# A hybrid encoder layer on one core: first transfers reordered, products of ones ahead of the data, rstd rows by way of DRAM, HGRN scores of two blocks issued together

## The chip, the cores and the metric

The kernel runs on one core of a Trainium2 chip. TensorE (PE) multiplies, VectorE (DVE), ScalarE (ACT) and GpSimd (POOL) do elementwise work, and SyncE (SP) issues the DMAs. The metric is the device time in microseconds of one execution; the median of the kernel before is 2376.36 us.

## The reference, cut to what matters

One layer is applied to two sequences, a prompt of 512 tokens and a sample of 1024. The model width is 1024, everything is float32.

```python
h = rms_norm(x, n_pre_mix)
proj = h @ w_in                       # width 6672
qkv_g, z_g, a_g, b_g, q_h, f_h, i_h, g_h, gate_raw = split(proj)
# branch A: bidirectional gated delta rule, 4 heads of 128, conv of 5 taps, chunks of 64
o_a = gated_delta(q, k, v, g[0], beta[0]) + flip(gated_delta(flipped ...))
y_a = (rms_norm(o_a) * silu(z_g)) @ w_br_gdn
# branch B: bidirectional HGRN2, 4 heads of 128
o_b = gla(qh, kh[0], ih, logf[0]) + flip(gla(flipped ...))
y_b = (rms_norm(o_b) * silu(g_h)) @ w_br_hg
merged = sigmoid(gates_0) * y_a + sigmoid(gates_1) * y_b
x = x + rms_norm(merged @ w_out, n_post_mix)
h2 = rms_norm(x, n_pre_ffn)
ff = (silu(h2 @ w_gate) * (h2 @ w_up)) @ w_down
return x + rms_norm(ff, n_post_ffn)
```

`gla` multiplies decayed queries and keys of one chunk into a triangular score matrix, applies it to the values, and carries a state from chunk to chunk.

## The kernel before, in words

**Tiles and stages.** The tokens form three blocks of 512: block 0 is the first sequence, blocks 1 and 2 are the second. Activations lie with features on the partitions, as eight 128x512 tiles per block (KD = 8). A product in full precision is made of three fp32r products of split operands: hi by hi, hi by lo, lo by hi. ACT rounds to the high part, DVE subtracts to get the low one (`split`). The mixer (projections, both branches, gates) takes about the first half of the span, then come the output projection and the feed-forward part, whose products use a seven-product Strassen scheme.

**An order written by a planner.** The program is first written as a tape. `Plan.run` interleaves five streams (prelude, GDN, HGRN, dense projections, output) by estimated times; a stream yields a time or a key and goes on when the plan has reached it. `Tape.schedule` (line 436) then simulates a list scheduler over the tape: each operation has a cost (line 289), an earliest time `o.rel` (0 at first, line 443) and a priority (its place on the tape), and each engine takes the ready operation of the best priority. It also assigns the buffers. `emit` (line 2599) writes the program in that order, and on the chip every engine runs its own list in order, with semaphores between engines.

**Units of small products.** `units` (line 416) binds products of the same small form into units that are emitted in one go. Line 423 lets an operation join the current unit only while the unit has newly opened at most two PSUM tiles (one, for full-size fp32 products). Lines 552 to 562 hold a unit of small products back by the number of instructions that PE was given in the last FETCH = 5000 ns: four for each fp32 product, two for others. With 64 products, a unit waits until the rest of the window holds at most 64.

**The start.** `layer` (line 766) loads the table of ACT (line 768) and makes the constants: `ones`, `ident`, masks; `vcol`, the 128x88 vector constants with all the gains, is loaded on SP (line 911). `prelude` (line 1155) then loads, for k = 0 to 7, the x tile and the w_ih tile (the HGRN value weights), each 256 KB, all on SP. With the entries of AHEAD (line 49) it also fetches 512 KB chunks of w_in early. `values(k)` (line 1180) converts x (scaled by the gain `g_mix`, a column of vcol) and w and multiplies them into four PSUM tiles, 12 products per k. After the first VSPLIT = 4 of them on the tape, `constants` and `ab_constants` follow (line 1193), small chains on DVE, ACT and POOL. The squares for the rms norm and their sums come next, at plan time TOKENS. Until rstd is known, projections use the unscaled x and are scaled when they are evicted; from plan time NORMED the x tiles are normalized one by one.

**rstd rows.** For blocks 1 and 2, `rstd_row` (line 1107) squares token rows, gets rstd as a column per 128 tokens, and spreads it to all partitions with four products ones x diag(y) on PE and a copy by ACT.

**HGRN.** `hg_stream` (line 1781) calls `hg_attn` (line 1793) for each head. For one block after the other it prepares four score operands per direction (`hg_pre`), multiplies the scores in 64 small products (16 of 32 rows by 64, 48 of 32 by 32, written to the PSUM tiles `pa` and `pb`), makes the state increments (`hg_post`) and selects the valid scores into SBUF. A small product is two instructions in the profile, so one block's burst has 128.

**Fillers.** `gates` (line 1731) and `dense_stream` (line 1743) give projections that can run at any time. HOLD (line 42) says how many gate chunks of a group go out early and how many wait for the inversion of the delta rule, MSTEP (line 43) at which of its steps that inversion counts as done.

Of the kernel before, what the change touches and what calls it, by code (L numbers as in the profile page):

```python
# [13 lines left out]
F32 = mybir.dt.float32  # L14
# [26 lines left out]
WBUFS = (2, 2, 2)  # L41
HOLD = ((2, 2, 1, 2), (2, 2, 2, 2))
MSTEP = (24, 28)
PAIR = False
# [3 lines left out]
NVEC = 88  # L48
AHEAD = {4: 512, 6: 1536, 7: 2064}
VSPLIT = 4  # L50
TRIG = 0
TOKENS, NORMED = 22.0, 30.0
QSQ = P * EPS ** 0.5
# [3 lines left out]
class Op:  # L57

    __slots__ = ("idx", "eng", "meth", "args", "kw", "occ", "dur", "tiles", "need", "succ", "rel", "prio", "form", "unit",
                 "asked", "port", "part")  # L60
# [103 lines left out]
class Tape:  # L164
# [29 lines left out]
    def __init__(self, nc):  # L194
        self.nc = nc
        self.fake = bacc.Bacc("TRN2", target_bir_lowering=False, num_devices=1)
        for n in self.ENGS:
            setattr(self, n, Tape.Eng(self, n))
        self.ops = []
        self.vts = {}  # L200
        self.pools = {}
        self.masks = {}
        self.cuts = {}
        self.count = 0
        self.part = (0, False)
        self.shift = 0

    def apart(self, pairs=False):
# [4 lines left out]
    @contextmanager  # L213
    def sooner(self, n):

        self.shift += n
        yield
        self.shift -= n

    def cut(self, name):  # L220
# [137 lines left out]
    def add(self, eng, meth, args, kw):  # L358
        o = Op()
        o.idx = len(self.ops)  # L360
        o.prio = o.idx - self.shift
        o.eng, o.meth, o.args, o.kw = eng, meth, args, kw
        o.form, o.unit, o.port, o.part = None, [o], 0, self.part
        out = args[0]
# [71 lines left out]
    def schedule(self):  # L436
# [4 lines left out]
        for o in ops:  # L441
            o.succ = []
            o.rel = 0.0
            o.asked = False
# [321 lines left out]
def layer(ctx, tc, x_p, x_s, w_out, n_post_mix, n_post_ffn, w_down, vec, xt_p, xt_s, w_in, w_br, w_gate, w_up,  # L766
# [52 lines left out]
    def dma(out, in_, eng=None):  # L819
        (eng or nc.sync).dma_start(out, in_)  # L820
        pl.dma(out, in_)
# [64 lines left out]
    def ctile(shape, name, dtype=F32):  # L886
        return const.tile(shape, dtype, name=name, tag=name)

    ident = ctile([P, P], "ident")
    nc.gpsimd.memset(ident, 0.0)  # L890
    nc.gpsimd.affine_select(ident, ident, [[-1, P]], ALU.not_equal, 1.0, base=0, channel_multiplier=1)
    ones = ctile([P, P], "ones")
    nc.vector.memset(ones, 1.0)
    ones_r = nc.tile(rpool, [P, P], F32R, "ones_r")
    eps_c = ctile([P, 1], "eps_c")
# [12 lines left out]
    for j in range(4):  # L908
        nc.gpsimd.memset(mbd[32 * j:32 * j + 32, 32 * j:32 * j + 32], 1.0)
    vcol = ctile([P, NVEC], "vcol")  # L910
    dma(vcol, vec)
    sgn, bwd, own, inc = [ctile([P, 1], n) for n in ("sgn", "bwd", "own", "inc_")]
# [194 lines left out]
    def rstd_row(blk_):  # L1107
# [13 lines left out]
        tt(y, y, u, ALU.mult)  # L1121
        pb = px()
        for t in range(4):
            dg = sblk("dg")
            ts(dg, ident, y[:, t:t + 1], ALU.mult)
            mm(t4(pb)[:, t, :], ones, dg)
        row = blk("row")
        copy(row, pb)
        rstd[blk_] = row
        yield 0  # L1130

    rstd = {}
    waiting = []

# [20 lines left out]
    def prelude(q):  # L1155
# [9 lines left out]
        if q.si == 0:  # L1165
            xt = []
            hi, lo = h_tiles()
            pv = [px() for t in range(4)]
            wr = []
            for k in range(KD):  # L1170
                xt.append(load(0, k))
                wr.append(blk("wv"))
                dma(wr[k], w_ih[k])
# [619 lines left out]
    def hg_attn(q, h):  # L1793
        out = q.hg[h]
        for b in range(q.nb):
            pa = px()
            pb = px()
            parts = [{}, {}]
            yield from par(*[hg_pre(h, out, b, d, parts[d]) for d in range(2)])
            pav, pbv = t4(pa), pb[:, 0:P].rearrange("p (t c) -> p t c", c=32)  # L1800
            halves = [slice(0, 64), slice(64, P)]
            yield pl.at(parts[0]["l64"], parts[1]["l64"], parts[0]["l32"], parts[1]["l32"])
            for t in range(4):
                for j in range(4):
                    d, sl = j // 2, slice(32 * j, 32 * j + 32)
                    dl = t4(parts[d]["l64"])
                    mm(pav[sl, t, halves[1 - d]], dl[:, t, sl], dl[:, t, halves[1 - d]])
            for d in range(2):
                e1, e2, l32 = [parts[d][n] for n in ("e1", "e2", "l32")]
                for t in range(4):  # L1810
                    for j in range(4):
                        sl = slice(32 * j, 32 * j + 32)
                        fs = slice(t * P + 32 * j, t * P + 32 * j + 32)
                        mm(pav[sl, t, sl] if d == 0 else pbv[sl, t, :], e2[:, fs], e1[:, fs])
                    for j in (0, 2):
                        ks, qs = [slice(32 * (j + z), 32 * (j + z) + 32) for z in (d, 1 - d)]
                        mm(pav[ks, t, qs], t4(l32)[:, t, ks], t4(l32)[:, t, qs])
# [4 lines left out]
            nc.vector.copy_predicated(av, m_all[:, None, :].to_broadcast([P, 4, P]), t4(pa))  # L1822
            pl.op("DVE", a_, [pa, a_])
            bd = sblk("bd").rearrange("p (t c) -> p t c", c=32)
            pset(bd, 0.0)
            nc.vector.copy_predicated(bd, m_b[:, None, :].to_broadcast([P, 4, 32]),
                                      pb[:, 0:P].rearrange("p (t c) -> p t c", c=32))
            pl.op("DVE", bd, [pb, bd])
            for j in range(4):
# [828 lines left out]
```

## Time and profile before

| what | us |
|---|---|
| median of 3 runs (2375.31 to 2376.83) | 2376.36 |
| the profiled execution | 2376.19 |
| its span, first to last instruction | 2374.5 |
| PE busy (14168 products) | 2359.3 |
| DVE busy | 1722.2 |
| ACT busy | 1244.3 |
| POOL busy | 753.7 |

The page gives busy times over the whole span. Products overlap on PE, and their ends are modelled, so the mean duration of a product is longer than the distance between two starts; how fast PE goes is read from counts in a window. Nearly all instructions have line 650, the planner's emit helper, so groups are told apart by their tiles: `bank` is PSUM, `ha` and `wa` hold split operands, `la`, `ba`, `sm`, `sa` are arenas of smaller tiles (`ones` lies in `sm`).

### The profile page before, as it was taken

Reading aid. Unit: us, or ns where it says so; the run is one execution under the profiler, and the core shown is the slowest. Engines: PE = TensorE matmul, PEld = TensorE weight load, DVE = VectorE, ACT = ScalarE, POOL = GpSimd, SP = SyncE. Lnnn points to the kernel's source line nnn. Section 1 sums busy time; section 2 is a strip of 40 time slices with the busy share of each in tenths; the row PEclk is TensorE's granted clock in tenths of the full one; section 3 lists DMA queues with packets and bytes.
Section 4 is the critical chain, followed back from the end, with each engine's and each line's share of the span. In section 5 each row is a group of like instructions: output and inputs, shape, how many; then the busy total and the mean of one; then the engine's idle time right before and its main releaser. Section 6 shows DMA issues by size and latency. Waiting matters only on the chain.

```text
span 2374.5 us, 37882 instructions
## 1 busy us (share of the span) xinstructions
PE 2359.3 (99%) x14168; PEld 1974.5 (83%) x14168; DVE 1722.2 (73%) x2826; ACT 1244.3 (52%) x2159; POOL 753.7 (32%) x1019
## 2 busy tenths in 40 slices
PE   8999999999999999999999999999999999999998
PEld 7888888888888888888888888888888888888887
DVE  6798789858848968759856885656787887544566
ACT  6766766746637647538442464545344444433343
POOL 0534524331602612502400011124676665200221
PEclk9999999999999999999999999999999999999999
DMA  6542343221320311325874463452455544674463
GB/s 224 173 134 87 123 134 92 94 81 45 108 77 23 112 67 54 100 75 173 281 258 157 159 212 118 152 173 77 167 192 177 178 159 173 217 244 138 148 205 128
DMA packets 194071, 337.72 MB, mean 142 GB/s; under 512 B 53248, under 2 KB 93024, under 8 KB 193888
## 3 DMA queue, kind: packets, MB, share of 16 engines
q1 hardware_dynamic: 193888, 335.31, 42.4%
q8 instruction: 111, 1.82, 0.3%
q14 instruction: 72, 0.59, 0.1%
HBM read 254.59 MB, written 80.66 MB: 141 GB/s over the span
## 4 chain that ended last, share of the span: by engine, by line
PE 98%; DVE 1%; ACT 0%; issue 0%; POOL 0%; DVEq 0%; POOLq 0%
PE bank L650 98%; DVE la_a L650 1%; DVE ba_a L650 0%; DVE wa_a L650 0%; ACT la_a L650 0%; ACT wa_a L650 0%; DVE da_a L650 0%; DVE sm_a L650 0%; POOL sm_a L650 0%; DVE sa_a L650 0%; POOL la_a L650 0%; ACT ba_a L650 0%; DVEq L2653 0%; ACT ha_a L650 0%; POOL sa_a L650 0%
## 5 line engine op out<-in xcount | busy, mean ns | idle before, releaser
L650 PE MATMUL bank<-ha_a,wa_a 128*128 128x512 f32 x5328 | 1278.7, 394 | 0.0
L650 PEld LDWEIGHTS bank<-ha_a,wa_a 128*128 128x128 f32 x5328 | 985.1, 188 | 196.5 <-issue 1.3
L650 PE MATMUL bank<-xr_a 128*128 128x512 f32 x1386 | 314.3, 389 | 0.0
L650 POOL TENSOR_TENSOR ba_a<-ba_a 128x512 f32<-128x512 f32 (+1 forms) x121 | 164.2, 1361 | 453.7 <-DVE sa_a L650 211.2
L650 PEld LDWEIGHTS bank<-xr_a 128*128 128x128 f32 x1386 | 260.3, 188 | 53.8
L650 PE MATMUL bank<-xr_a,ha_a 128*128 128x512 f32 x1200 | 275.3, 389 | 0.0
L650 PEld LDWEIGHTS bank<-xr_a,ha_a 128*128 128x128 f32 x1200 | 225.4, 188 | 46.6
L650 ACT ACTIVATE la_a<-la_a 128x512 f32<-128x512 f32 (+1 forms) x324 | 204.9, 647 | 56.8 <-DVE la_a L650 42.5
L650 DVE TENSOR_TENSOR wa_a<-ba_a,wa_a 128x1024 fp32r<-128x1024 f32 (+1 forms) x109 | 128.3, 1180 | 117.2 <-PE bank L650 76.4
L650 DVE TENSOR_TENSOR wa_a<-la_a,wa_a 128x1024 fp32r<-128x1024 f32 (+1 forms) x119 | 138.1, 1164 | 70.3 <-PE bank L650 41.0
L650 ACT ACTIVATE wa_a<-ba_a 128x1024 fp32r<-128x1024 f32 (+1 forms) x109 | 105.5, 969 | 154.3 <-PE bank L650 133.5
L650 ACT ACTIVATE wa_a<-la_a 128x1024 fp32r<-128x1024 f32 (+1 forms) x119 | 115.4, 974 | 127.8 <-PE bank L650 120.0
L650 ACT ACTIVATE ha_a<-ba_a 128x512 fp32r<-128x512 f32 (+1 forms) x124 | 79.7, 645 | 151.1 <-PE bank L650 115.3
L650 PE MATMUL bank<-wa_a,ha_a 128*128 128x512 f32 x624 | 144.2, 393 | 7.5 <-ACT wa_a L650 7.5
L650 DVE TENSOR_TENSOR la_a<-la_a 128x512 f32<-128x512 f32 (+2 forms) x200 | 138.4, 705 | 12.2 <-ACT la_a L650 11.5
L650 PEld LDWEIGHTS bank<-wa_a,ha_a 128*128 128x128 f32 x624 | 118.5, 190 | 32.2 <-ACT wa_a L650 7.5
L650 DVE TENSOR_TENSOR ha_a<-ba_a,ha_a 128x512 fp32r<-128x512 f32 (+1 forms) x124 | 125.9, 1021 | 13.9 <-ACT ha_a L650 13.7
L650 DVE TENSOR_TENSOR xr_a<-da_a,xr_a 128x1024 fp32r<-128x1024 f32 (+2 forms) x60 | 71.1, 1199 | 64.1 <-ACT xr_a L650 44.0
L650 POOL TENSOR_TENSOR la_a<-la_a 128x256 f32<-128x256 f32 (+1 forms) x63 | 62.8, 1011 | 172.2 <-DVE la_a L650 79.4
L650 ACT ACTIVATE xr_a<-da_a 128x1024 fp32r<-128x1024 f32 (+2 forms) x60 | 58.5, 987 | 106.2 <-PE bank L650 105.9
L650 PE MATMUL bank<-ha_a 128*128 128x512 f32 x480 | 112.1, 389 | 0.0
L650 PEld LDWEIGHTS bank<-ha_a 128*128 128x128 f32 x480 | 90.2, 188 | 18.6
(209 smaller groups left out, 3312.5 us busy)
## 6 DMA issues: line engine op xcount, KB each, us to landing
la_a<-lay_w_in SPq DMA_DIRECT2D x62, 512.0 KB
ba_a<-lay_w_in SPq DMA_DIRECT2D x38, 512.0 KB
ba_a<-lay_w_gate SPq DMA_DIRECT2D x35, 512.0 KB
ba_a<-lay_w_up SPq DMA_DIRECT2D x34, 512.0 KB
dram_a_sc<-xa_a SPq DMA_DIRECT2D x55, 256.0 KB
ba_a<-w_ffn_down SPq DMA_DIRECT2D x23, 512.0 KB
da_a<-dram_a_sc SPq DMA_DIRECT2D x22, 512.0 KB
ba_a<-dram_a_sc SPq DMA_DIRECT2D x20, 512.0 KB
```

Of the source, the lines that this page charges most:

```text
L650: f(*[m(a) for a in o.args], **{k: m(a) for k, a in o.kw.items()})
```

## The change

- **First transfers.** The first w_ih tile goes first, vcol moves from SP to ACT's queue, the first x tile is the second load on SP. For k = 0 the x tile is converted and multiplied in two halves of 256 tokens, and the weights are split before x.
- **Products of ones.** Nine fp32 products ones x ones go into a PSUM tile ahead of everything else on PE. Their result is not used.
- **Later constants.** VSPLIT is 8, so all value products stand before the constants on the tape. Constants and squares get an earliest time of 6000 ns in the planner (LATER).
- **rstd rows.** y is written to DRAM as 4x128 elements and read back as a 512-element row broadcast to all partitions. The four products, the diagonals and the copy go.
- **HGRN scores.** `hg_attn` prepares both directions of all blocks of the sequence first, then issues the scores of all blocks, then does the rest block by block. For the first sequence, with one block, nothing changes.
- **Planner numbers.** HOLD, MSTEP, AHEAD, TOKENS and NORMED get other values.

```diff
-HOLD = ((2, 2, 1, 2), (2, 2, 2, 2))
-MSTEP = (24, 28)
+HOLD = ((1, 1, 2, 1), (2, 3, 3, 1))
+MSTEP = (26, 29)
...
-AHEAD = {4: 512, 6: 1536, 7: 2064}
-VSPLIT = 4
+AHEAD = {2: 512, 4: 1536, 6: 2064}
+VSPLIT = 8
+LATER = 6000.0
...
-TOKENS, NORMED = 22.0, 30.0
+TOKENS, NORMED = 26, 50
...
+    @contextmanager
+    def later(self, t):
+
+        old, self.after = self.after, t
+        yield
+        self.after = old
...
+        o.after = self.after
...
-            o.rel = 0.0
+            o.rel = o.after
...
+    w0 = pl.tile(tp, [P, TB + 4], F32, "wv", "t", TBUFS)[:, 0:TB]
+    dma(w0, w_ih[0])
+    vcol = ctile([P, NVEC], "vcol")
+    dma(vcol, vec, nc.scalar)
+    x0 = pl.tile(gp, [P, TB], F32, "xt", "xt", 8)
+    halves = [slice(z * 2 * P, (z + 1) * 2 * P) for z in range(2)]
+    dma(x0, xt_p[0:P, 0:TB])
...
     nc.vector.memset(ones, 1.0)
+    warm = pl.tile(psx, [P, TB], F32, "px", "px", 5)
+    for t in range(9):
+        mm(warm[:, 0:P], ones, ones)
...
-    vcol = ctile([P, NVEC], "vcol")
-    dma(vcol, vec)
...
-        pb = px()
-        for t in range(4):
-            dg = sblk("dg")
-            ts(dg, ident, y[:, t:t + 1], ALU.mult)
-            mm(t4(pb)[:, t, :], ones, dg)
+        sc = r_sc[blk_ - 1]
+        dma(sc.rearrange("t p -> p t"), y)
         row = blk("row")
-        copy(row, pb)
+        dma(row, bass.AP(tensor=sc.tensor, offset=sc.offset, ap=[[0, P], [1, TB]]))
...
+    r_sc = [dram.tile([4, P], F32, name="r_sc%d" % i) for i in range(2)]
...
             def values(k):
-                act(hi[:, k, :], xt[k], AF.Copy, scale=g_mix[:, k:k + 1])
                 hl = pl.tile(wsp, [P, 1024], F32R, "whl", "whl", 6)
                 wh, wl = hl[:, 0:TB], hl[:, TB:2 * TB]
-                split(wh, wl, wr[k])
-                stt(lo[:, k, :], xt[k], g_mix[:, k:k + 1], hi[:, k, :].bitcast(F32), ALU.mult, ALU.subtract)
-                for x, w in ((hi, wh), (hi, wl), (lo, wh)):
-                    for t in range(4):
-                        mm(pv[t], x[:, k, t * P:(t + 1) * P], w, k == 0 and w is wh and x is hi, k == KD - 1 and x is lo)
+                if k == 0:
+                    split(wh, wl, wr[k])
+                for z in halves if k == 0 else [slice(0, TB)]:
+                    act(hi[:, k, z], xt[k][:, z], AF.Copy, scale=g_mix[:, k:k + 1])
+                if k:
+                    split(wh, wl, wr[k])
+                for z in halves if k == 0 else [slice(0, TB)]:
+                    stt(lo[:, k, z], xt[k][:, z], g_mix[:, k:k + 1], hi[:, k, z].bitcast(F32), ALU.mult, ALU.subtract)
+                for ts_ in ((0, 1), (2, 3)) if k == 0 else (range(4),):
+                    for x, w in ((hi, wh), (hi, wl), (lo, wh)):
+                        for t in ts_:
+                            mm(pv[t], x[:, k, t * P:(t + 1) * P], w, k == 0 and w is wh and x is hi, k == KD - 1 and x is lo)
...
-            constants()
-            ab_constants()
+            with nc.later(LATER):
+                constants()
+                ab_constants()
...
-            for k in range(KD):
-                act(sq[k], xt[k], AF.Square)
+            with nc.later(LATER):
+                for k in range(KD):
+                    act(sq[k], xt[k], AF.Square)
...
     def hg_attn(q, h):
         out = q.hg[h]
+        parts = [[{}, {}] for b in range(q.nb)]
         for b in range(q.nb):
-            pa = px()
-            pb = px()
-            parts = [{}, {}]
-            yield from par(*[hg_pre(h, out, b, d, parts[d]) for d in range(2)])
...
+            yield from par(*[hg_pre(h, out, b, d, parts[b][d]) for d in range(2)])
+        ps = [(px(), px()) for b in range(q.nb)]
+        pav = [t4(p[0]) for p in ps]
+        pbv = [p[1][:, 0:P].rearrange("p (t c) -> p t c", c=32) for p in ps]
+        halves = [slice(0, 64), slice(64, P)]
+        yield pl.at(*[parts[b][d][n] for b in range(q.nb) for d in range(2) for n in ("l64", "l32")])
+        for b in range(q.nb):
             for t in range(4):
                 for j in range(4):
                     d, sl = j // 2, slice(32 * j, 32 * j + 32)
-                    dl = t4(parts[d]["l64"])
-                    mm(pav[sl, t, halves[1 - d]], dl[:, t, sl], dl[:, t, halves[1 - d]])
+                    dl = t4(parts[b][d]["l64"])
+                    mm(pav[b][sl, t, halves[1 - d]], dl[:, t, sl], dl[:, t, halves[1 - d]])
...
-            yield from par(*[hg_post(out, b, d, parts[d]) for d in range(2)])
+        for b in range(q.nb):
+            yield from par(*[hg_post(out, b, d, parts[b][d]) for d in range(2)])
             a_ = ht_("pa", 2)
```

More of the change, by code (lines that the diff above doesn't have):

```diff
@@ L57 @@
 class Op:
-    __slots__ = ("idx", "eng", "meth", "args", "kw", "occ", "dur", "tiles", "need", "succ", "rel", "prio", "form", "unit",
+    __slots__ = ("idx", "eng", "meth", "args", "kw", "occ", "dur", "tiles", "need", "succ", "rel", "after", "prio", "form", "unit",
                  "asked", "port", "part")
@@ L206, in __init__ @@
         self.shift = 0
+        self.after = 0.0
     def apart(self, pairs=False):
@@ L1165, in prelude @@
         if q.si == 0:
-            xt = []
+            xt = [x0]
             hi, lo = h_tiles()
             pv = [px() for t in range(4)]
-            wr = []
+            wr = [w0]
             for k in range(KD):
-                xt.append(load(0, k))
-                wr.append(blk("wv"))
-                dma(wr[k], w_ih[k])
+                if k:
+                    xt.append(load(0, k))
+                    wr.append(blk("wv"))
+                    dma(wr[k], w_ih[k])
                 if k in AHEAD:
@@ L1180, in values @@
             def values(k):
-                act(hi[:, k, :], xt[k], AF.Copy, scale=g_mix[:, k:k + 1])
                 hl = pl.tile(wsp, [P, 1024], F32R, "whl", "whl", 6)
                 wh, wl = hl[:, 0:TB], hl[:, TB:2 * TB]
-                split(wh, wl, wr[k])
-                stt(lo[:, k, :], xt[k], g_mix[:, k:k + 1], hi[:, k, :].bitcast(F32), ALU.mult, ALU.subtract)
-                for x, w in ((hi, wh), (hi, wl), (lo, wh)):
-                    for t in range(4):
-                        mm(pv[t], x[:, k, t * P:(t + 1) * P], w, k == 0 and w is wh and x is hi, k == KD - 1 and x is lo)
+                if k == 0:
+                    split(wh, wl, wr[k])
+                for z in halves if k == 0 else [slice(0, TB)]:
+                    act(hi[:, k, z], xt[k][:, z], AF.Copy, scale=g_mix[:, k:k + 1])
+                if k:
+                    split(wh, wl, wr[k])
[5 more added lines that the diff above has]
+                            mm(pv[t], x[:, k, t * P:(t + 1) * P], w, k == 0 and w is wh and x is hi, k == KD - 1 and x is lo)
             for k in range(VSPLIT):
@@ L1794, in hg_attn @@
         out = q.hg[h]
+        parts = [[{}, {}] for b in range(q.nb)]
         for b in range(q.nb):
-            pa = px()
-            pb = px()
-            parts = [{}, {}]
-            yield from par(*[hg_pre(h, out, b, d, parts[d]) for d in range(2)])
-            pav, pbv = t4(pa), pb[:, 0:P].rearrange("p (t c) -> p t c", c=32)
-            halves = [slice(0, 64), slice(64, P)]
-            yield pl.at(parts[0]["l64"], parts[1]["l64"], parts[0]["l32"], parts[1]["l32"])
+            yield from par(*[hg_pre(h, out, b, d, parts[b][d]) for d in range(2)])
[5 more added lines that the diff above has]
+        for b in range(q.nb):
             for t in range(4):
@@ L1805, in hg_attn @@
                     d, sl = j // 2, slice(32 * j, 32 * j + 32)
-                    dl = t4(parts[d]["l64"])
-                    mm(pav[sl, t, halves[1 - d]], dl[:, t, sl], dl[:, t, halves[1 - d]])
+                    dl = t4(parts[b][d]["l64"])
+                    mm(pav[b][sl, t, halves[1 - d]], dl[:, t, sl], dl[:, t, halves[1 - d]])
             for d in range(2):
-                e1, e2, l32 = [parts[d][n] for n in ("e1", "e2", "l32")]
+                e1, e2, l32 = [parts[b][d][n] for n in ("e1", "e2", "l32")]
                 for t in range(4):
@@ L1813, in hg_attn @@
                         fs = slice(t * P + 32 * j, t * P + 32 * j + 32)
-                        mm(pav[sl, t, sl] if d == 0 else pbv[sl, t, :], e2[:, fs], e1[:, fs])
+                        mm(pav[b][sl, t, sl] if d == 0 else pbv[b][sl, t, :], e2[:, fs], e1[:, fs])
                     for j in (0, 2):
                         ks, qs = [slice(32 * (j + z), 32 * (j + z) + 32) for z in (d, 1 - d)]
-                        mm(pav[ks, t, qs], t4(l32)[:, t, ks], t4(l32)[:, t, qs])
-            yield from par(*[hg_post(out, b, d, parts[d]) for d in range(2)])
+                        mm(pav[b][ks, t, qs], t4(l32)[:, t, ks], t4(l32)[:, t, qs])
+        for b in range(q.nb):
+            yield from par(*[hg_post(out, b, d, parts[b][d]) for d in range(2)])
             a_ = ht_("pa", 2)
@@ L1821, in hg_attn @@
             pset(a_, 0.0)
-            nc.vector.copy_predicated(av, m_all[:, None, :].to_broadcast([P, 4, P]), t4(pa))
-            pl.op("DVE", a_, [pa, a_])
+            nc.vector.copy_predicated(av, m_all[:, None, :].to_broadcast([P, 4, P]), pav[b])
+            pl.op("DVE", a_, [ps[b][0], a_])
             bd = sblk("bd").rearrange("p (t c) -> p t c", c=32)
             pset(bd, 0.0)
-            nc.vector.copy_predicated(bd, m_b[:, None, :].to_broadcast([P, 4, 32]),
-                                      pb[:, 0:P].rearrange("p (t c) -> p t c", c=32))
-            pl.op("DVE", bd, [pb, bd])
+            nc.vector.copy_predicated(bd, m_b[:, None, :].to_broadcast([P, 4, 32]), pbv[b])
+            pl.op("DVE", bd, [ps[b][1], bd])
             for j in range(4):
```

## The prediction

> **What bounds the kernel now.** I read the page first (busy time, slices, chain), then the waits of PE, then the timeline of the first 32 us, then the places in the middle that the change touches. From the page:
>
> ```profile
> PE 2359.3 (99%) x14168; PEld 1974.5 (83%) x14168; DVE 1722.2 (73%) x2826; ACT 1244.3 (52%) x2159; POOL 753.7 (32%) x1019
> PE   8999999999999999999999999999999999999998
> PE 98%; DVE 1%; ACT 0%; issue 0%; POOL 0%; DVEq 0%; POOLq 0%
> ```
>
> The waits of PE are two lines (total, times, longest):
>
> ```profile
> PE bank L650 <- ACT wa_a L650: 7.5, 1, 7.5
> PE bank L650 <- DVE wa_a L650: 0.2, 1, 0.2
> ```
>
> So PE is the bound from its first product to its last. The span of 2374.5 us is 7.5 us in which PE waits for its first operands, 2359.3 us of products and about 7.7 us after them. DVE, ACT and POOL have 27% and more to spare. The time can change by three things only: when the first product starts, how much PE time the program asks for, and whether a new hole opens in PE's stream. An edit that only shifts DVE or ACT work costs nothing as long as PE keeps a queue of ready products.
>
> The start, from the timeline (start, duration, engine):
>
> ```profile
> 0.80 1.28 ACT L768 ACT_TABLE_LOAD   x1 [0.80 <-PEq L2648]
> 0.80 0.39 SPq L650 DMA_DIRECT2D sa_a<-lay_vec  x1
> 0.90 0.17 DVE L650 MEMSET sm_a<- 128x128 f32 x1 [0.90 <-PEq L2648]
> 1.24 0.42 SPq L650 DMA_DIRECT2D la_a<-lay_xt_prompt  x1
> 1.71 0.43 SPq L650 DMA_DIRECT2D la_a<-lay_w_ih  x1
> ...
> 2.09 0.21 ACT L650 ACTIVATE sm_a<-sa_a 128x16 f32<-128x16 f32 x1
> ...
> 5.63 0.21 ACT L650 ACTIVATE sa_a<-sa_a 128x8 f32<-128x8 f32 x1 [2.71 <-DVE sa_a L650]
> 5.75 0.71 ACT L650 ACTIVATE ha_a<-la_a,sa_a 128x512 fp32r<-128x512 f32 x1
> ...
> 6.36 0.61 ACT L650 ACTIVATE la_a<-la_a 128x512 f32<-128x512 f32 x1
> ...
> 6.88 0.61 ACT L650 ACTIVATE wa_a<-la_a 128x512 fp32r<-128x512 f32 x1
> ...
> 7.55 8.63 PE L650 MATMUL bank<-wa_a,ha_a 128*128 128x512 f32 x28 [7.55 <-ACT wa_a L650]
> ```
>
> ACT stands 2.71 us behind a tiny exponential of the constants, whose operand DVE delivers last. Then it makes the high part of x (5.75), a square that nobody needs yet (6.36), and the high part of the weights (6.88). The first product follows at 7.55. Were the data there earlier? The DMA view of the windows 0 to 3.75 us and 0 to 4.8 us:
>
> ```profile
> DMA packets 332, 0.40 MB, mean 108 GB/s; under 512 B 157, under 2 KB 157, under 8 KB 332
> DMA packets 518, 0.75 MB, mean 155 GB/s; under 512 B 176, under 2 KB 176, under 8 KB 518
> ```
>
> Each 256 KB tile is 128 packets of 2 KB. There were 332 - 157 = 175 of them by 3.75 and 518 - 176 = 342 by 4.8, so the 256 packets of the first two tiles were through at about 4.3 (interpolated). ACT, not the DMA, was late.
>
> **The change at the start.** The first weights, then the first x, now go first on SP, and vcol goes on ACT's queue; the constants and squares are held back; the first x tile is converted in halves. I estimate the first weights at 3.7 us and x at 4.3 to 4.7 with the landing signal. ACT converts the weights (0.61) before x is in. The half tile costs between 0.21 (128x16) and 0.71 (128x512); linear in the width, 0.45. Data products could start at 4.8 to 5.2. vcol is 44 KB. Its packets were in by 3.75 (they are most of the 157 under 512 B). If ACT issues it only after its table load (2.08 instead of 0.80), it is in by 5.0 at the latest and the data products start by 5.5; nothing else is queued on ACT then.
>
> Ahead of them stand nine products of ones. Their price needs the rate of PE, here by windows (PE, PEld, DVE, ACT, POOL busy with counts, then granted clock, DMA share, GB/s):
>
> ```profile
> 7.55:11.75 4.20, 4.20 (x10) 3.33 (x11) 3.63 (x6) 4.20 (x8) 0.00 (x0) 1.00 1.03 386
> 15.79:31.50 15.71, 15.71 (x70) 12.77 (x68) 6.35 (x8) 7.31 (x11) 0.00 (x0) 1.00 1.01 403
> ```
>
> The first ten products take 0.42 us each, the later ones 15.71 / 70 = 0.224, though the granted clock reads 1.00 in both rows. PE runs at half rate for its first 4.2 us, and that costs 10 x 0.196 = 2.0 us. The nine products of ones need only the memset on DVE (0.90 + 0.17), so they start at about 1.15. One fp32 product is two instructions, and eight such instructions take 89.81 - 89.00 = 0.81 us (rows in the next part). Eighteen take 1.8 us at full rate and 3.6 to 4.0 at half rate, so PE is free for data at 4.8 to 5.2, just when the data come. I put the first data product at 5.3 us: a gain of 7.55 - 5.3 = 2.25. The half-rate time of 4.2 us then ends at about 5.35. I allow 0.3 us of it to be paid by data products: a gain of 2.0 - 0.3 = 1.7. If nothing of the warm-up carries over, this term is 0; if all does, 2.0.
>
> The Trainium skill (TensorE: Matmul & The Clock Gate, Part 1) says that PE starts at half clock and gets the full one after a busy window of about 3.4 us that runs freely, not from the kernel's start. The 4.2 us above agree with it. By its worst phase (two windows, 6.8 us after 1.15) data products would run at half rate until 7.95, six of them, and the term would be 0.8 instead of 1.7; this is an estimate from that page.
>
> Supply afterwards: at full rate PE eats a 512 KB pair (x and weights of one k) in 12 x 0.224 = 2.7 us, and the DMA brings 512 KB in 1.3 us at the 403 GB/s above. ACT needs 0.71 + 0.61 per pair. So the earlier loading of w_in chunks (AHEAD) and the tail of constants fit in. Should the second pair be late, the cost is the gap, up to 0.5 us.
>
> **rstd rows.** Per block of the second sequence, four fp32 products ones x diagonal (eight instructions) go:
>
> ```profile
> 89.00 1.06 PE L650 MATMUL bank<-sm_a 128*128 128x128 f32 x8
> 89.81 2.57 PE L650 MATMUL bank<-ha_a,wa_a 128*128 128x512 f32 x10
> ...
> 137.82 1.06 PE L650 MATMUL bank<-sm_a 128*128 128x128 f32 x8
> ```
>
> That is 0.81 us each, at most 1.06, so 1.6 to 2.1 for both; I take 1.7. In their place come two DMAs per block, a write of 512 single elements and a broadcast read that waits on SP for the write. The nearest rows are another round trip through DRAM:
>
> ```profile
> 71.08 4.16 SPq L650 DMA_DIRECT2D dram_u_sc<-la_a  x8
> ...
> 76.58 1.98 SPq L650 DMA_DIRECT2D ba_a<-dram_u_sc  x4
> ```
>
> The reads go out 76.58 - 75.24 = 1.3 us after the last write was issued. One row should hold SP for about as long, bounded by 0 and the 5.5 us of this whole exchange. Behind it stand the loads of x and w_in. A w_in chunk feeds PE for 24 x 0.224 = 5.4 us, and one chunk is in hand while the next is fetched. So I cost it at nothing; without that cover it is up to 5.5 us per row.
>
> **HGRN scores.** One burst of a block:
>
> ```profile
> 1128.24 1.52 PE L650 MATMUL bank<-ha_a,wa_a 128*128 128x512 f32 x6
> 1129.70 0.25 PE L650 MATMUL bank<-la_a 128*32 128x64 f32 x2
> ...
> 1130.17 1.17 PE L650 MATMUL bank<-la_a 128*32 128x32 f32 x96
> 1131.27 1.42 PE L650 MATMUL bank<-ha_a,wa_a 128*128 128x512 f32 x5
> ```
>
> The sixth big product starts at 1128.24 + 5 x 0.224 = 1129.36, and the burst 0.34 later instead of 0.224: 0.1 us to enter. At the exit five products take 1.42 where the six before took 1.52, so 1.52 - 0.224 = 1.30 was due: another 0.1. The last small product may drain for about 0.1 more. Two bursts run as one would save 0.2 to 0.3 us per head, 1.2 us over four heads. But I do not expect them to run as one. The order is made in units, and `units()` (line 423) closes a unit of small products at its third new PSUM tile. Two blocks open four (pa and pb of each), so the unit breaks where the second block begins. Lines 555 to 562 then push a unit of 64 products back until its predecessors of the last 5 us hold at most 64 instructions, and the first unit alone counts 256. So I expect two bursts of 128 instructions per head, some 5 us apart, and a gain of 0.
>
> **The planner's numbers.** HOLD, MSTEP, NORMED and TOKENS move which ready product comes next, not how many there are. NORMED at 50 instead of 30 keeps the raw x for 20 us more, some four chunks, and so gives DVE four more scalings of an eviction, each like these:
>
> ```profile
> L650 DVE TENSOR_TENSOR la_a<-la_a 128x512 f32<-128x512 f32 (+2 forms) x200 | 138.4, 705 | 12.2 <-ACT la_a L650 11.5
> ```
>
> 4 x 0.705 = 2.8 us on an engine with 27% idle: nothing. The bound is -0.2 (the one wait left after the start) to +2 us, the largest single wait that I would expect a new order to open.
>
> **Sum.** -2.25 - 1.7 - 1.7 = -5.65 us. The profiled execution took 2376.19 us, so 2370.5; the median of the three runs stands 0.17 higher, so 2370.7. I write 2370.6. A measurement of this kernel tells about 0.2%, 4.75 us, from no change; the forecast is just past that.
>
> **Rivals.**
>
> One burst after all: if the break is not made, or the two units come out back to back, 1.2 us more go: 2369.4. For it speaks that the diff's loops write both blocks' products directly behind each other, against it the two places in the code.
>
> The warm-up does not carry over: products of ones finish before the rate changes, or the wait for data after them resets it. Then 1.7 us come back: 2372.3, no measurable difference. For it speaks that the trace shows only one warm-up, with data products; against it that ones and data products are the same instruction to PE. The skill's free-running window, above, lands in between, at 2371.5.
>
> Slower, by the scores: both blocks are now prepared before either is multiplied, with four PSUM tiles held, and the whole work after the scores of both lies behind the second burst. In the last head PE goes from the burst (1129.70) to the end of the head's chain:
>
> ```profile
> 1149.96 2.43 PE L650 MATMUL bank<-ha_a,wa_a 128*128 128x512 f32 x10
> 1152.60 0.51 PE L650 MATMUL bank<-wa_a,ra_a 128*128 128x512 f32 x1 [0.21 <-DVE wa_a L650]
> ```
>
> That is 22.9 us for the chain, and PE has its only wait after the start at its end, so the cover is thin there. A block's share is half, 11.4 us. If PE has no other product for it, the time is 2370.6 + 11.4 = 2382. It decides from 5.7 us exposed upwards. Against it: in the three other heads PE never waits, and the projections of the second phase can fill in.
>
> SP held too long: the write of a rstd row has 512 elements, four times the 128 rows of vcol, which were in by 3.75, at most 2.95 us after their issue. Four times that is 11.8 us, 1.0 more than the two chunks in hand last (2 x 5.4 = 10.8). Two rows then cost 2 us: 2372.6. Slower than before it gets from 13.6 us per row. Nothing here shows 4-byte data packets, so the size is open. The Trainium skill (DMA: Bandwidth & Descriptors, Rules for kernel authors) warns against transposing by a plain DMA with a rearranged pattern and names a factor of 19; at 19 times the 1.3 us above, an estimate, the time would be 2398.
>
> **How the numbers follow.** Forecast 0.58, one burst 0.13, no carry-over 0.15, slower by the scores 0.10, SP held 0.04. Of the forecast about 0.52 lies more than 4.75 us under the median; with the one-burst case that makes faster 0.65. No carry-over (0.15), the rest of the forecast (0.06), half of the SP case (0.02) and a partly covered scores case (0.02) make same 0.25; slower is 0.10. The range takes in the one-burst case with 1.2 us below it and no carry-over with 1.5 us above: 2368.2 to 2373.8. It leaves out most of the two last cases, 0.13, and little else.
>
> **What would show it.** Right: products of ones from about 1.2 us; the first data product at 5 to 5.5 us; products near 0.23 us from the first or second on; the last of the 96 first products at about 27 us (today 31.5); no 128x128 products from sm_a alone after that; four pairs of score bursts in the second sequence, each pair some 5 us apart. Wrong: a PE wait between the ones and the data of over 1 us; 0.42 us per product after 6 us; PE waits of over 1 us between 590 and 1160 us, or on a DMA of x_sample or w_in near 90 and 140 us; a score group of 256 instructions.

## The result, and the profile after

The changed kernel takes 2391.68 us (median of 6 runs, 2390.16 to 2395.52), the kernel before 2376.60 beside it (6 runs): a ratio of 1.0066, 95% interval 1.0055 to 1.0076. It is slower by 15 us where I forecast 6 us faster, and outside the range. The profiled execution took 2391.91 us, its span is 2390.2.

From the page of the kernel after (busy time, slices, chain):

```profile
PE 2364.2 (99%) x14170; PEld 1975.5 (83%) x14170; DVE 1725.8 (72%) x2823; ACT 1242.3 (52%) x2158; POOL 746.1 (31%) x1019
PE   9989999999999999999999999999999999999998
PE 93%; DVE 3%; DMA 2%; ACT 1%; issue 0%; SPq 0%; DVEq 0%
```

PE is still the bound. It is busy 4.9 us longer than before, 3.9 of them with products of ones, although the half-rate start and the rows' products are gone. The third slice is no longer a 9, and PE's share of the chain is 93% instead of 98%. The waits of PE (total, times, longest) were two lines before; now they are:

```profile
PE bank L660 <- DVE ba_a L660: 7.5, 1, 7.5
PE bank L660 <- DVE la_a L660: 4.0, 3, 1.5
PE bank L660 <- ACT wa_a L660: 3.1, 1, 3.1
PE bank L660 <- issue: 2.1, 1, 2.1
PE bank L660 <- DVE sm_a L660: 1.3, 2, 1.1
PE bank L660 <- DVE wa_a L660: 0.5, 1, 0.5
PE bank L660 <- ACT ha_a L660: 0.2, 1, 0.2
```

Only 1.3 us of these are the start. The start itself came as forecast (timeline: start, duration, engine):

```profile
0.80 0.38 SPq L660 DMA_DIRECT2D la_a<-lay_w_ih  x1
0.82 0.39 ACTq L660 DMA_DIRECT2D sa_a<-lay_vec  x1
...
1.12 3.90 PE L660 MATMUL bank<-sm_a 128*128 128x128 f32 x18 [1.12 <-DVE sm_a L660]
...
5.22 8.50 PE L660 MATMUL bank<-wa_a,ha_a 128*128 128x512 f32 x36 [0.20 <-ACT ha_a L660]
```

The first data product starts at 5.22 (forecast 5.3), and the first 36 go at full rate from the first on: 8.50 / 36 = 0.236 us each, where before the first ten took 0.42. So the 15 us come from later. The largest waits lie behind the two rstd rows of the second sequence. The same view from 89 us on:

```profile
89.20 0.38 SPq L660 DMA_DIRECT2D dram_r_sc<-sm_a  x1
...
89.67 0.93 SPq L660 DMA_DIRECT2D ba_a<-x_sample  x2
...
99.62 0.33 SPq L660 DMA_DIRECT2D ba_a<-dram_r_sc  x1
...
102.15 1.06 ACT L660 ACTIVATE ba_a<-ba_a 128x1024 f32<-128x1024 f32 x1 [7.10 <-DMA ba_a<-x_sample]
...
109.08 0.38 SPq L660 DMA_DIRECT2D dram_r_sc<-sm_a  x1
...
110.05 0.43 SPq L660 DMA_DIRECT2D ba_a<-lay_w_in  x1
...
120.98 0.32 SPq L660 DMA_DIRECT2D la_a<-dram_r_sc  x1
121.34 0.43 SPq L660 DMA_DIRECT2D la_a<-lay_w_in  x1
...
122.36 1.06 ACT L660 ACTIVATE wa_a<-ba_a 128x1024 fp32r<-128x1024 f32 x1 [9.27 <-DMA ba_a<-lay_w_in]
...
123.47 0.77 PE L660 MATMUL bank<-ha_a,wa_a 128*128 128x512 f32 x2 [3.06 <-ACT wa_a L660]
...
124.73 4.02 PE L660 MATMUL bank<-ha_a,wa_a 128*128 128x512 f32 x11 [0.49 <-DVE wa_a L660]
...
136.22 0.65 PE L660 MATMUL bank<-ba_a,la_a 32*32 32x32 f32 x32 [7.47 <-DVE ba_a L660]
```

Read it from SP. The write of a row goes out at 89.20, the read that needs it at 99.62. The second pair stands at 109.08 and 120.98. A write of 2 KB takes 10.4 and 11.8 us to land, and SP stands for 18.9 of these 22.3 us (total, times, longest):

```profile
SPq L660 <- DMA dram_r_sc<-sm_a: 18.9, 2, 9.9
```

Loads issued behind it come late too: the x tile of 89.67 reaches ACT at 102.15, the w_in chunk of 110.05 at 122.36. The next chunk can be issued only at 121.34, behind the read. PE runs out at 123.47 - 3.06 = 120.4. The windows view shows why the loads are late (columns as in the prediction; the last three are granted clock, DMA share, GB/s). The first line is the kernel before, the other two are after:

```profile
89.00:99.00 10.00, 10.00 (x52) 8.43 (x51) 6.02 (x13) 8.62 (x18) 8.28 (x23) 1.00 0.42 135
89.00:99.00 10.00, 10.00 (x48) 8.33 (x47) 4.64 (x6) 5.96 (x10) 8.48 (x20) 1.00 0.94 31
109.00:120.50 11.50, 11.41 (x77) 8.81 (x76) 5.18 (x9) 3.37 (x6) 0.00 (x0) 1.00 0.94 55
```

In after the 16 DMA engines are 94% busy while 31 and 55 GB/s move; in before they moved 135 GB/s at 42%. From 89.20 to 99.62, 528 of the 607 packets are under 512 bytes, and the row has 512 elements. So the single elements occupy the engines, not only SP.

The scores stand in two bursts per head, as forecast. Those of one head lie before and behind the second of these rows, with 5.74 us of other products between them:

```profile
973.74 6.28 PE L660 MATMUL bank<-ha_a,wa_a 128*128 128x512 f32 x27
...
981.52 5.74 PE L660 MATMUL bank<-ha_a,wa_a 128*128 128x512 f32 x24
```

### The profile page after: what moved, and what is told of

Its sections match the earlier page's. It is cut to its first block, busy times and chain, and to the rows that moved or that the text cites. A ratio compares the mean times of both kernels' runs of the same rounds, so it can differ in the third digit from the quotient of the medians.

```text
span 2390.2 us, 37935 instructions
## 1 busy us (share of the span) xinstructions
PE 2364.2 (99%) x14170; PEld 1975.5 (83%) x14170; DVE 1725.8 (72%) x2823; ACT 1242.3 (52%) x2158; POOL 746.1 (31%) x1019
## 4 chain that ended last, share of the span: by engine, by line
PE 93%; DVE 3%; DMA 2%; ACT 1%; issue 0%; SPq 0%; DVEq 0%
PE bank L660 93%; DVE la_a L660 1%; DVE ba_a L660 1%; DMA ba_a<-x_sample 1%; DMA dram_r_sc<-sm_a 0%; DMA la_a<-x_sample 0%; DVE sm_a L660 0%; DVE wa_a L660 0%; ACT la_a L660 0%; DMA la_a<-lay_w_in 0%; ACT ba_a L660 0%; SPq L660 0%; DMA la_a<-lay_xt_prompt 0%; ACT wa_a L660 0%; DVE ha_a L660 0%
## 5 line engine op out<-in xcount | busy, mean ns | idle before, releaser
L660 ACT ACTIVATE la_a<-la_a 128x512 f32<-128x512 f32 (+1 forms) x312 | 198.8, 650 | 74.3 <-DVE la_a L660 44.0
L660 DVE TENSOR_TENSOR wa_a<-ba_a,wa_a 128x1024 fp32r<-128x1024 f32 (+1 forms) x113 | 136.5, 1209 | 98.9 <-PE bank L660 57.3
L660 ACT ACTIVATE wa_a<-ba_a 128x1024 fp32r<-128x1024 f32 (+1 forms) x113 | 110.7, 980 | 163.2 <-PE bank L660 147.8
L660 POOL TENSOR_TENSOR la_a<-la_a 128x256 f32<-128x256 f32 (+2 forms) x64 | 69.9, 1107 | 374.4 <-DVE sa_a L660 205.8
L660 ACT ACTIVATE wa_a<-la_a 128x1024 fp32r<-128x1024 f32 (+1 forms) x115 | 110.5, 965 | 128.6 <-PE bank L660 98.8
L660 DVE TENSOR_TENSOR la_a<-la_a 128x512 f32<-128x512 f32 (+2 forms) x192 | 126.5, 673 | 8.7 <-ACT la_a L660 7.3
L660 ACT ACTIVATE ba_a<-ba_a 128x512 f32<-128x512 f32 (+1 forms) x152 | 95.8, 639 | 21.6 <-DVE ba_a L660 7.8
```

The lines of the kernel that those rows point to most:

```text
L660: f(*[m(a) for a in o.args], **{k: m(a) for k, a in o.kw.items()})
```

## The experiments

Theory 1: the row's write holds up SP and the DMA engines; the rest is free. Theory 2: the new order itself, which the planner draws anew after any edit, opens waits of 0.5 to 3 us that the planner doesn't foresee. Some edits were therefore made with the order of before (or after) kept instruction by instruction and single instructions exchanged at emission; these are called pinned. The expectations of the later runs call theory 2 theory 4, and theory 3 is that the scores lengthen the chain of each head. Times are medians, ratios are to the kernel before on the same chip (2376.2 to 2376.6).

**Rows back on PE, in after.** The hunk of `rstd_row` is taken out of after; the planner draws a new order.

```diff
-        dma(sc.rearrange("t p -> p t"), y)
...
+            mm(t4(pb)[:, t, :], ones, dg)
...
+        copy(row, pb)
```

> The changed kernel with the rstd rows made on PE again, nothing else undone. Theory 1, the element write: each write of 512 single elements takes 10 to 12 us, the loads behind it come that much later, and PE has two holes (3.1 us at 123, 7.5 us at 136) with some 4 us of half-rate products after them. Then both holes go, 1.7 us of products come back, and the time is 2391.7 - 10.6 - 0.7 - 4 + 1.7 = about 2378. Theory 2, the new order (HOLD, MSTEP, NORMED): the holes come from what the planner puts where, and stay: 2390 or more.

Measured: 2391.88, 1.0066 [1.0051, 1.0081]. The waits at 123 and 136 us are gone, others came, 14.2 us in all after the start, of which these two lines are the largest:

```profile
PE bank L660 <- issue: 5.8, 2, 3.0
PE bank L660 <- DVE la_a L660: 3.0, 3, 1.6
```

So theory 1 alone can't be the whole cause, and the 2378 expected from it was far off.

**Rows through DRAM alone, in before.** The same hunk, the other way, on before.

> The kernel before with only the rstd rows taken through DRAM. Theory 1: two element writes of 10 to 12 us, PE holes between about 90 and 150 us, 2376.6 - 1.7 + 5 to 15 = 2380 to 2390. Theory 2: no hole, 1.7 us of products fewer, 2375.

Measured: 2388.99, 1.0052 [1.0037, 1.0067], with a wait of 7.80 us at 132.7. Most of the loss comes with the rows alone; here too the order was new.

**New score loops alone, in before.** `hg_attn` of after.

> The kernel before with only the scores of both blocks issued behind one another. Theory 3, the scores lengthen the chain of each head of the second sequence: PE waits of 1.5 to 2.2 us appear between 590 and 1160 us as in the changed kernel (1.5 at 1009.7, 2.2 at 1145.8), 2376.6 + 3 to 5 = 2380 to 2382. Theory 2, those waits come from HOLD and MSTEP: 2376 to 2377. Both: the bursts stay two per head, about 7 us apart.

Measured: 2382.75, 1.0026 [1.0017, 1.0035]. Waits after the start: 4.3 us, 2.8 of them issue (in which nothing in the profile holds PE). The largest, 1.60, stands at the second burst of the last head, where after has its issue wait of 2.06 (at 1145.8). The eight products behind the 1.60 take 3.65 us, at half rate.

**Start alone.** After without the row and score hunks and with the old HOLD and MSTEP.

> The changed kernel with the rstd rows on PE, the scores block by block, and HOLD and MSTEP of before: what is left is the start (first transfers, products of ones, later constants) with its AHEAD, TOKENS and NORMED. The start alone is worth 7.55 - 5.22 = 2.3 us of waiting and 2.0 us of half rate: 2376.6 - 4.3 = 2372.3. If the new TOKENS, NORMED or AHEAD open a hole, as the 1.1 us wait at 61.7 in the changed kernel may be, it is 2373 to 2374.

Measured: 2383.01, 1.0028 [1.0017, 1.0040]. The start is there, and 7.5 us of waits at nine later places eat more than its gain.

**Pinned start.** Before's order; nine products of ones first on PE, and the constants' chain and the square moved behind the first weights' split.

```diff
-        nc.emit(order)
+        for o in order:
+            if o.idx in (38, 102, 103, 104, 105, 106, 107, 108, 196):
+                held.append(o)
...
+            if o.idx == 2:
+                for t in range(9):
+                    tc.nc.tensor.matmul(real[bank, last][:, 0:P], nc.real(ones), nc.real(ones), start=True, stop=True)
```

> The kernel before in its own order of instructions, instruction by instruction, with only this done to it when it is written out: nine products of ones at the head of PE, and the first square, the chain of the lower bound and the low part of the first x moved behind the low part of the first weights. Theory 4: the start is worth what was forecast and everything that the changed kernel lost comes from its new order. Then the first data product is at 5.5 us instead of 7.55, no product after it is at half rate, no new PE wait appears, and the time is 2376.6 - 2.0 - 2.0 = 2372.6. Rival: the start has a price of its own later (supply, clock): 2376 or more.

Measured: 2373.38, 0.9988 [0.9979, 0.9998]. Waits of PE:

```profile
PE bank L2611 <- DVE sm_a L650: 1.1, 1, 1.1
PE bank L650 <- ACT wa_a L650: 0.7, 2, 0.4
```

No later wait opens. The start is worth 3.0 us if the order stays.

**Pinned rows.** Before's order; each row's products, diagonals and copy exchanged for the single-element write and the broadcast read.

> The kernel before in its own order, with only the rstd rows' products and copies replaced, at their places, by the element write and the broadcast read. Theory 1: the write alone, 10 to 12 us with the loads behind it held up, opens the holes: two PE waits of 3 to 8 us near 95 and 145 us, half-rate products after the longer ones, 2376.6 - 1.7 + 5 to 14 = 2380 to 2389. Theory 4 without theory 1 (only the new order costs): 2375.

Measured: 2385.70, 1.0040 [1.0026, 1.0054]. Nothing but the rows moved, and they cost 9.4 us. The timeline where the first row is needed:

```profile
88.86 2.99 PE L650 MATMUL bank<-ha_a,wa_a 128*128 128x512 f32 x12
...
96.29 0.37 SPq L2607 DMA_DIRECT2D la_a<-r_sc  x1
...
99.43 1.08 PE L650 MATMUL bank<-sa_a,la_a 128*128 128x128 f32 x4 [7.58 <-DVE la_a L650]
```

The row's write goes out at 77.27, ahead of loads that the kernel before issues at 80.12 and 85.54. Here they go out at 88.62 and 95.39, and the read stands behind them. The second row is written at 106.90 and read 36 us later, and only a wait of 0.37 us follows it.

**HOLD and MSTEP alone, in before.**

> The kernel before with only HOLD and MSTEP of the changed one: the same products, another order. Theory 4 (a new order opens holes that the planner does not foresee): 2 to 6 us of PE waits, 2379 to 2383. Rival (HOLD and MSTEP are harmless): 2376 to 2377.

Measured: 2382.69, 1.0026 [1.0017, 1.0036]. The work is the same to the product (14168), and yet:

```profile
PE bank L650 <- ACT wa_a L650: 9.1, 2, 7.5
PE bank L650 <- DVE ba_a L650: 1.6, 3, 0.6
PE bank L650 <- DVE la_a L650: 0.8, 1, 0.8
PE bank L650 <- issue: 0.4, 1, 0.4
```

The 7.5 is the start of before. The others lie at 352, 421, 643, 818, 1002 and 1005 us; after has waits at 430 and 1010.

**SLACK 620.** The planner's allowance for SP 600 to 620 ns: an edit that asks for nothing.

> The kernel before with one number of the planner moved by nothing that matters: it takes 620 ns instead of 600 ns as the safety behind a DMA. The tape is the same, some 1800 of PE's instructions change places by one or two. Theory 4 in its strong form (any new order costs, the kernel before is a lucky draw): 2378 to 2381. In its weak form (only far-reaching changes of the order cost): 2376 to 2377.

Measured: 2377.63, 1.0005 [0.9996, 1.0014], with 1.4 us of new waits. A small redraw can be nearly free.

**NORMED 31.** Another such edit: the retention of the raw x tiles, 30 to 31 us.

> The kernel before with one planner number changed by a thirtieth (the retention of the raw x tiles 30 to 31 us), nothing else: a second redraw of the order that asks for no other work. Theory A (a redraw opens waits of its own): 2378 to 2384, new PE waits of 0.5 to 2 us at unrelated places. Theory B (a redraw alone is free, as the one with the slack of 620 nearly was): 2375.5 to 2377.5.

Measured: 2383.44, 1.0030 [1.0019, 1.0042]. So it can also cost 7 us. Besides the start there are 4.6 us of waits, seven of them, from 70 to 819 us, the longest 1.1.

**After with the write priced.** The planner believes that the write takes 2.2 us; here it is told 10.2.

```diff
-            o.form = rows * max(run * 4, 512) / self.RATE
+            o.form = rows * (20 if run == 1 else max(run * 4, 512) / self.RATE)
```

> After with one number of the planner changed: a DMA of single elements is priced at 20 ns per element (10.2 us for the row's write instead of 2.2), so that its order counts with the 10 to 12 us that the trace of after shows. Theory A (the planner's ignorance of this write makes the holes at 123 and 136 us, and work to cover it exists): the two holes of 3.1 and 7.5 us go, 2380 to 2383, with the scattered waits of the redrawn order left. Theory B (the write holds up the loads behind it, whatever the order knows, and there is no work to cover it): the plan itself has 10 us of PE idle between 134 and 142 us, so holes of the same size stand there, 2388 to 2393.

Measured: 2398.89, 1.0099 [1.0082, 1.0116], above both ranges. Theory B's holes are there, 4.4 + 2.8 + 0.8 + 0.6 us from 135 to 142, and a new wait of 4.75 at 1238. Told the price, the planner found no cover in this order.

**Scores as one burst.** New score loops in before, and the limit of a unit raised so that 256 instructions per head go in one piece.

```diff
-... len(fresh | new) <= (1 if o.form == self.FULL and not o.part[1] else 2)
+... len(fresh | new) <= (1 if o.form == self.FULL and not o.part[1] else 4)
```

> The kernel before with the new score loops, and with the planner's limit for a unit of small products raised from two new PSUM tiles to four, so that both blocks of a head go as one burst of 256 instructions. Theory A (a burst costs its entry and its exit, 0.1 to 0.2 us each): four entries and exits fewer than in the run with the new loops alone, so 1.2 us under its 2382.75, some 2381.5. Theory B (dense small products run the engine out of instructions): an issue wait of 1.5 to 3 us behind most of the four long bursts, 2385 to 2395. Theory C (each redrawn order opens its own waits of 0.5 to 3 us): 2380 to 2388, waits in new places, several of them away from the scores.

Measured: 2398.61, 1.0095 [1.0080, 1.0110]. The waits of PE and the windows across the first long burst:

```profile
PE bank L650 <- issue: 14.2, 5, 4.0
```

```profile
608.00:614.00 6.00, 6.00 (x28) 4.83 (x26) 0.00 (x0) 3.32 (x5) 5.06 (x13) 1.00 0.11 44
614.16:616.40 2.24, 2.24 (x198) 2.24 (x200) 0.56 (x2) 0.00 (x0) 1.85 (x6) 1.00 0.12 43
```

Each of the four bursts has an issue wait of 1.8 to 3.7 us in or behind it, and the last a second one of 4.0. In the burst PE takes 398 instructions in 2.24 us, against 54 in 6 us before. Issue waits were 2.8 us in the run with 128 instructions at a time, 1.6 of them at a burst, and none in before, which has bursts of 128 too. So the long bursts bring these waits, and here the longer burst brings more. That the supply of instructions runs dry fits, as one packet of some 16 KB on an instruction queue moves in or shortly before each of these waits, but it is not shown; no record says what PE waits for. The raised limit also holds for other small products, and the order is new.

**Pinned lines.** As pinned rows, with another form of write: one PE transpose turns the 128x4 tile, ACT copies it, and four lines of 512 bytes are written. The edit against pinned rows:

```diff
-        swap[a] = lambda y=y, sc=sc: tc.nc.sync.dma_start(sc.rearrange("t p -> p t"), nc.real(y))
+        swap[a + 1] = lambda y=y, pb=pb: turn(y, pb)
+        swap[z - 2] = lambda pb=pb, dg=dg, sc=sc: spread(pb, dg, sc)
```

> The order of before kept instruction for instruction; each rstd row is made by one PE transpose of the 128x4 tile, an ACT copy of 4x128, a write of four 512-byte lines to DRAM and a broadcast read, instead of four products of ones with diagonals. It differs from the run with the single-element write in the write's form (and in one transpose and one copy). Theory A (the 10 to 12 us of the single-element write make the hole of 7.6 us): no hole over 1 us at 90 to 150 us, 2374.5 to 2376. Theory B (any trip through DRAM at this place is too long for the work queued behind it): a hole of 3 to 8 us again, 2380 to 2386.

Measured: 2375.75, 1.0000 [0.9990, 1.0009]: 10 us better than pinned rows. The same place:

```profile
90.16 0.28 SPq L2609 DMA_DIRECT2D r_sc<-sm_a  x1
...
91.47 0.33 SPq L2615 DMA_DIRECT2D la_a<-r_sc  x1
...
92.45 0.60 PE L650 MATMUL bank<-sa_a,la_a 128*128 128x128 f32 x4
```

The read goes out 1.31 us after the write, and PE doesn't wait. The trip through DRAM is harmless in this form. The write also stands later than in pinned rows (90.16 against 77.27), so this pair alone doesn't separate the form from the place; the last run does.

**Pinned start and lines.**

> The order of before kept, with the new start and with the rstd rows by four 512-byte lines. If the start is worth 3.0 us and the line write has no hole: 2371.5 to 2373. If the line write has a hole too: 2377 to 2383. If the rows' products were covered anyway: 2373.4 as with the start alone.

Measured: 2372.31 (10 runs, 2371.45 to 2375.01), 0.9985 [0.9976, 0.9994]. It beats both kernels, by less than 0.2% though its interval excludes 1, and the gain over the pinned start is not resolved.

**After with lines.** After's own order kept; DVE turns the tile in 32x32 blocks, and SP writes four pieces in runs of 128 bytes.

```diff
+        tc.nc.vector.transpose(b, a)
+        for g in range(4):
+            tc.nc.sync.dma_start(nc.real(sc[:, 32 * g:32 * g + 32]), b[32 * g:32 * g + 4])
```

> After in its own order, every instruction at its place, except that the write of each rstd row is made in long runs: DVE turns the 128x4 tile in 32x32 blocks (three small DVE instructions) and SP writes four pieces of 4x32 elements in 128-byte runs instead of 512 single elements. Theory A (of after's 15 us over before, the single-element write makes the holes of 3.1 and 7.5 us and the half-rate products behind them, and the redrawn order makes the rest): these two holes go, 2377 to 2381. Theory B (with the order fixed, the loads behind the row are late for whatever form of write): holes of 5 us or more stay there, 2386 to 2392. Theory C (the write is the whole loss and the redraw costs nothing): 2371 to 2374.

Measured: 2380.18 (10 runs, 2376.68 to 2384.19), 1.0017 [1.0007, 1.0026]. This is theory A: the form of the write is 11.5 of after's 15.1 us (11.1 with each kernel measured against the one before beside it). SP's order is that of after, so the place is the same. Timeline and window of the first row, then the waits of PE:

```profile
93.74 1.28 SPq L2636 DMA_DIRECT2D dram_r_sc<-turn  x4
...
96.16 0.33 SPq L660 DMA_DIRECT2D ba_a<-dram_r_sc  x1
```

```profile
89.00:99.00 10.00, 10.00 (x48) 8.23 (x47) 7.63 (x16) 9.58 (x15) 8.51 (x20) 1.00 0.45 158
```

```profile
PE bank L660 <- DVE la_a L660: 5.6, 3, 2.6
PE bank L660 <- issue: 1.9, 1, 1.9
PE bank L660 <- DVE sm_a L660: 1.3, 2, 1.1
```

The DMA share falls from 0.94 to 0.45 while five times as much moves (158 against 31 GB/s). Counted from the write, 93.74 to 103.74, it is 0.73 at 224 GB/s. All waits from 123 to 137 us are gone. What stays after the start is 2.64 us at 64, 1.36 at 419, 1.62 at 999 and 1.90 (issue) at 1135. The first of these lies ahead of the rows, where after runs the same instructions and waits 1.07, so a part of it varies from execution to execution.

## Why the prediction was wrong

**The start, -2.25: right.** First data product at 5.22 instead of 5.3. The last of the 96 first products ends at 29.3 and not at 27, since nine projection products (9 x 0.224 = 2.0 us) now run among them; that work isn't lost.

**The warm-up, -1.7: right.** No data product of the start ran at half rate. My reason that ones and data are the same instruction was loose (a product of ones is two instructions of 128x128, a data product one of 128x512), but the warm-up carried over. Both terms together were 3.95; pinned, the start gave 3.0. That was a simpler form of the edit, with the first data product at 5.57, another wait of 0.26, and 1.45 us less of data products (2359.3 - (2361.9 - 4.05)).

**The rows' products, -1.7: about right, and small.** In the pinned kernel with lines PE is busy 1.1 us less (2358.2 against 2359.3), with a transpose left in; 1.3 us of new waits eat it.

**The rows' trip, "I cost it at nothing": failed, the largest error.** It took 11.5 us (after against after with lines). I had bounded SP's hold by 0 and 5.5 us, from an exchange of larger pieces. The rival "SP held too long" had the price, 11.8 us per write worked out from vcol's packets; measured are 10.4 and 11.8. That it came so close is partly luck, as vcol's 2.95 us was an upper bound with other loads beside it. Its cover was wrong. I set two chunks in hand against SP's wait alone. But the loads issued just behind the write share its DMA engines and come 12 us after their issue (89.67 to 102.15, 110.05 to 122.36), and the next chunk is not issued until SP is through. In place of 2 us for two rows, 3.06 + 0.49 + 7.47 = 11.0 us of waits came. The threshold of 13.6 us per row fell with that cover, and a chance of 0.04 was far too low for a price that my own nearest row put beyond the cover. The Trainium skill (DMA: Bandwidth & Descriptors, Rules for kernel authors) has a rule that I did not weigh: a last dimension that is not contiguous becomes one descriptor per element. The runs agree with it: the 512 single elements took 10.4 to 11.8 us, the same 2 KB in lines at most 1.31. The factor of 19 that I cited from there is at least 8 here (10.42 / 1.31).

**The scores, 0: right in the reading, too low in the price.** The unit breaks where I said. Yet the kernels with the new loops have an issue wait near the last head's second burst, 0.9 to 2.8 us (after 2.06, after with lines 1.90), and before and the kernels with the old loops have none there. My rival, an exposed chain of 11 us, did not happen. The rival of one burst had the wrong sign: built, it costs 15.9 us more than two bursts (2398.61 against 2382.75), 11.4 of them issue waits (14.2 - 2.8); the rest was not traced.

**The planner's numbers, "cost nothing, bound -0.2 to +2 us": failed, the second error.** HOLD and MSTEP alone cost 6.3 us, the start alone came out 10.7 above its expected 2372.3, and NORMED by one microsecond 7.2. I bounded the whole redraw by one wait; in these three runs and the one with the scores alone six to nine open, 4.3 to 7.5 us in all. In three of the four the granted clock also falls to 0.50 once behind them (at 226 us in the start alone, 230 in NORMED 31, 1135 in the scores alone). That a redraw always costs is not so: the slack edit cost 1.3, which its interval does not tell from nothing. Why before's order has only 0.2 us of waits after the start, while all but one of its redraws have 4 or more, stays open.

**The sum.** After with lines stands at 2380.18, 9.6 above my 2370.6. Its profiled span of 2379.2 is 10.3 above the forecast span (2374.5 - 5.65 = 2368.9). Waits after the start make 7.5 - 0.2 = 7.3 of that, and most of the rest is PE's busy time. Some 0.8 us of it are products at half rate from 65.72 us (15 in 4.18 us, against 15 x 0.224 = 3.36); the remainder was not traced. The pieces were not found by adding the single edits, which each redrew the order: rows, scores, start and HOLD/MSTEP alone lost 12.4, 6.2, 6.4 and 6.3 us against before, 31 in all, and after lost 15. Two of the signs that I had named for being wrong came: waits of PE behind late loads of w_in, near 123 to 136 us, and waits of over 1 us at 1010 and 1146.

## What to carry to other kernels

Price a DMA by its number of runs as well as its bytes, and count the loads queued behind it as delayed by the same time: 2 KB in 512 elements stopped a core's loads for 10 us, and turning the tile first cost nothing measurable. In a kernel whose order comes from a planner and has almost no idle time left on its bound engine, an edit also redraws the order, so test it once with the old order pinned before judging what the edit itself is worth. Here a redraw cost 1 to 7 us without any change in the number of products, so it deserves a term of several microseconds, not zero.

## What the hardware showed unexpectedly

**The clock can fall back after short waits.** Windows of after behind the waits of 3.06 and 7.47 us, then of after with lines behind its wait of 2.64 us (granted clock third from the end):

```profile
123.50:128.50 5.00, 4.51 (x13) 3.17 (x13) 3.55 (x5) 2.64 (x5) 2.29 (x3) 0.66 0.86 261
136.80:142.00 5.20, 5.20 (x67) 3.77 (x60) 4.69 (x13) 1.26 (x2) 2.50 (x6) 0.59 0.43 151
```

```profile
65.72:69.90 4.18, 4.18 (x15) 3.34 (x15) 3.41 (x9) 4.18 (x15) 0.00 (x0) 0.68 0.00 0
```

Eleven products took 4.02 us at 124.73 (0.365 each, against 0.224), so such a wait is paid again in part by the products behind it. In after with lines the clock reads 1.00 up to 65 us and 0.50 from 65 to 68. The length of the wait does not decide it alone: behind 1.60 us in the scores alone (1134.24) it fell to 0.50, behind 2.98 us in the run with the rows back on PE (423.23) and 2.06 us in after (1145.81) it stayed at 1.00. The Trainium skill (TensorE: Matmul & The Clock Gate, Part 1) puts the fall to half clock after an idle window of about 3.4 us. Here 1.60 us sufficed once and 2.98 us did not another time; the measurement decides. What else decides it is not shown.

**Products of ones warm the clock as data do.** Eighteen instructions ran in 3.90 us, and the 36 data products behind them at 0.236 us each, where the first ten of before took 0.42. This is read from the rates, as the granted clock reads 1.00 in both.
